# The first layer's FFN down with seven products for eight, its sum turned by TensorE, and another order of the last products

## The chip, the cores and the metric

The kernel runs on one core of a Trainium2 chip. The metric is the device time of one execution, in microseconds. The profile gives the engines these names: PE is TensorE (its loads of the stationary operand are PEld), DVE is VectorE, ACT is ScalarE, POOL is GpSimd, SP is SyncE, which here only issues DMAs.

## What is computed

Two layers of a decoder trunk on one sequence of 512 tokens with 1024 features. Each layer mixes four branches (a gated convolution, sparse attention, a gated recurrence, attention into 256 memory tokens), adds the result to `x`, and then applies an FFN:

```python
hf = rmsnorm(x, norm_ffn)
gate, up = jnp.split(hf @ ffn_w_up, 2, axis=-1)
return x + (jax.nn.silu(gate) * up) @ ffn_w_down
```

`ffn_w_up` is 1024 x 5632, `ffn_w_down` is 2816 x 1024. The change is in the last product, `(...) @ ffn_w_down`: a matrix of 512 tokens x 2816 times one of 2816 x 1024. Its 2816 rows are 22 K tiles of 128.

## The kernel before

**Products.** Each operand is split into a hi part, which TensorE's f32r format holds, and a lo part, the rest. A product of two operands is three matmuls (`mm3`, lines 275 to 277): hi x hi, hi x lo, lo x hi, added up in one bank of PSUM. ACT makes the hi part (line 97, the helper `A`), DVE the lo part (line 230 in `Chunk`, line 1068 in `split`). The tiles `w_hi` and `w_lo` have three buffers of 128 x 1024 (`W_BUFS`), the raw weights `w_raw` two. SP's queue loads the raw weights. PSUM's eight banks are three `mm`, three `tr` and two `at`.

**Who sets the order.** The program is written in one order, and a planner (the scheduler of the tile framework) puts each engine's instructions into an order of its own, by a timeline that it computes, by priorities (`tc.high_priority`), and by the dependences between tiles. Each engine then works strictly in that order. `tc.add_manual_dep(..., order, ...)` adds an order without a wait; `follow` (line 1058) uses it.

**The FFN** (`ffn`, from line 1172) goes in two parts of its 11 blocks of 256 hidden features: blocks 0 to 5, then 6 to 10 (`parts`). For each block, `features` multiplies eight K tiles of `h` with the gate's and the up's weights (96 matmuls of 128 x 512), DVE scales what comes out of PSUM (line 1208, `fg` and `fu`), ACT applies Silu, DVE multiplies (line 1211). When a part has its blocks, its share of the down product follows.

**Down, first layer** (`add_down`, line 1032). The hidden features are kept feature-major as `a_hi` and `a_lo` (lines 1215 and 1216). For each two chunks of 128 output features (`m0`) the weights of the part's K tiles are loaded and split, and `features` multiplies them: output features on the partitions, 512 tokens along the row. The sum in PSUM is added to a chunk of `x` that POOL's queue has brought back from DRAM (`x_c`, lines 1181 and 1043), and ACT's queue stores it (line 1046). That is done in both parts, 22 x 8 x 3 matmuls in all. In the second part each chunk at once becomes the next layer's `h` (`h_chunk`: hi part on ACT, lo part on DVE, line 289, and the squares' sum `ssq`, line 297).

**Down, last layer** (`down`, from line 1104). Here two K tiles form a 2 x 2 block problem: the two K tiles against the two halves of the tokens, and the two K tiles against the two halves of the output features. Eight block products become seven (a Strassen-Winograd scheme). `operands` (line 1085) makes seven combinations of 128 x 256 from a block's two feature tiles; `weight_sums` (line 1073) makes four combinations of a K pair's weights: POOL's queue loads the pair into `w_raw7` (line 1076), DVE does four subtractions (lines 1079 to 1082), POOL's queue stores them to `wt_dram` (line 1083), from which SP loads them again (lines 1132 and 1157). The hidden features are the stationary operand, so tokens come out on the partitions, and the result is added into the token-major `acc` (128 x 4 x 1024) by DVE (`evict`, line 1241). `x` enters `acc` beforehand, turned by TensorE (`x_in`, line 1190).

`down` runs in three stretches over the part's pairs. In the last one each pair `k` has a product into `ba` (two banks `mm`, called "main" below) and one into `bc` (two banks `at`), from one split of two weights:

```python
prod(ba, k, S3, p7, False, k == n - 1, True)
late.append((bc, k, S4, p3, False, k == n - 1, True))
if not n - 3 <= k < n - 1:
    for q in late:
        prod(*q)
    late = []
```

So as written, the products into `bc` of the pairs n-3, n-2 and n-1 come after the last product into `ba`; in the trace of before the planner has put each pair's behind its own main product. Then `evict` empties `ba` twice (into two halves of `acc`) and `bc`; in the last part of the last layer those of `bc` go out in halves of 256 columns, each followed by its transfer to the output (line 1244).

Of the kernel before, what the change touches and what calls it, by code (L numbers as in the profile page):

```python
# [21 lines left out]
P = 128  # L22
# [47 lines left out]
def hybrid_trunk(ctx: ExitStack, tc: tile.TileContext, x, mem, positions, norm_mix, w_in, conv_w,  # L70
# [41 lines left out]
    def f(ap):  # L112
        return ap.bitcast(F32)
# [127 lines left out]
    def wchunk(src, kt, n):  # L241
        return Chunk(src, kt, n)
# [29 lines left out]
    def mm3(ps, a, b, first, last, more=False):  # L272
        ah, al = a
        bh, bl = b
        pe.matmul(ps, ah, bh, start=first, stop=False, skip_group_check=more)  # L275
        pe.matmul(ps, ah, bl, start=False, stop=False, skip_group_check=more)  # L276
        pe.matmul(ps, al, bh, start=False, stop=last, skip_group_check=more)  # L277

    x_dram = nc.dram_tensor("x_spill", [P, KD, S], F32, kind="Internal").ap()
    wt_dram = nc.dram_tensor("w_sums", [P, FF // 256, 4, 512], F32, kind="Internal").ap()  # L280
# [751 lines left out]
    def add_down(x_chunk, w2d, a, kt, h2, ssq2, gain):  # L1032
        for m0 in range(0, KD, 2):
            ws = [(k0, wchunk(w2d[k0 * P:min(k0 + 8, kt) * P, m0 * P:(m0 + 2) * P], min(8, kt - k0), 256))
                  for k0 in range(0, kt, 8)]
            xs = [x_chunk(m0 + j) for j in range(2)]
            pss = [mm_ps() for _ in range(2)]
            for js in ([range(2)] if m0 + 2 < KD else [[0], [1]]):
                for k0, w in ws:
                    features(w, a, js, k0, kt, [pss[j] for j in js])  # L1040
            for j, xc in enumerate(xs):
                m = m0 + j
                dve.tensor_add(xc, xc, pss[j])
                if h2 is not None:
                    h_chunk(h2, ssq2, m, gain(m), xc)
                nc.scalar.dma_start(x_dram[:, m, :], xc)
# [26 lines left out]
    def weight_sums(fp, w2d, i):  # L1073

        raw = fp.tile([P, 4, 512], F32, name="w_raw7")
        nc.gpsimd.dma_start(raw.rearrange("p (e c) n -> p e (c n)", e=2),
                            w2d[2 * i * P:2 * (i + 1) * P, :].rearrange("(e p) n -> p e n", p=P))
        b12, b11, b22, b21 = (raw[:, j, :] for j in range(4))
        dve.tensor_sub(b11, b12, b11)
# [3 lines left out]
        nc.gpsimd.dma_start(wt_dram[:, i], raw)  # L1083

    def operands(fp, g0, g1):

        hi, lo = (fp.tile([P, 7, HALF], F32R, name=nm, bufs=6) for nm in ("a_hi", "a_lo"))
# [16 lines left out]
    def down(fp, w2d, sums, ops, evict):  # L1104
# [49 lines left out]
        for i0 in range(0, n, 2):  # L1154
# [17 lines left out]
    def ffn(l, h, ssq):  # L1172
# [3 lines left out]
        parts = ((0, 6), (6, n_f))  # L1176

        with tc.tile_pool(name="ffn", bufs=1, reuse_waits="tile") as fp:
# [14 lines left out]
            h2 = ssq2 = None  # L1193
            for part, (f0, f1) in enumerate(parts):
                ops = []
                if not last:
                    kt = 2 * (f1 - f0)
                    a = (fp.tile([P, 12, S], F32R, name="a_hi")[:, :kt], fp.tile([P, 12, S], F32R, name="a_lo")[:, :kt])
                if last:
                    weight_sums(fp, ffn_w_down[l], f0)  # L1200
                for fc in range(f0, f1):
# [10 lines left out]
                    if not last:  # L1212
                        for j, g in enumerate(gs):
                            i = 2 * (fc - f0) + j
                            A(a[0][:, i, :], g, AF.Copy)
                            dve.tensor_sub(a[1][:, i, :], g, f(a[0][:, i, :]))
                        continue
# [9 lines left out]
                if not last:  # L1227
                    if final:
                        h2, ssq2 = new_h(), new_ssq()
                    add_down(x_chunk, wd, a, kt, h2, ssq2, lambda c: g_mix(l + 1, c))  # L1230
                    continue
# [15 lines left out]
                down(fp, wd, wt_dram[:, f0:f1], ops, evict)  # L1247
        return h2, ssq2
# [34 lines left out]
```

## Time and profile before

| what | value |
|---|---|
| median of three runs | 2037.27 us (2035.32 to 2040.52) |
| the profiled execution | 2037.88 us |
| its span in the profile | 2036.2 us |
| mean granted TensorE clock | 0.997 |
| PE busy | 2017.4 us |
| DVE busy | 1356.6 us |
| ACT busy | 1046.3 us |
| first layer's FFN, first up product to the next layer's first product | 696.52 to 1056.54 us |
| last layer's FFN, first up product to the end of its products | 1680.70 to 2029.97 us |

The span runs from the first to the last instruction or transfer of one profiled execution; the time of that execution holds 1.7 us more. Rows of groups read: line, engine, operation, output tile from input tiles, shapes, count, then busy time in all, mean duration in ns, and idle time before. Rows of a timeline read: start in us, duration in us, engine, line, operation, tiles, shapes, count, and in brackets the idle time before it with what ended it.

### The profile page before, as it was taken

The page shows a single profiled execution, that of the slowest core. Times are in us where ns is not written, and L with a number is a line of the kernel's source. Part 1 is how long each engine was busy: PE and PEld are TensorE (multiplying, and loading weights), DVE is VectorE, ACT ScalarE, POOL GpSimd, SP SyncE. Part 2 cuts the span into 40 slices and gives each one's busy share as a digit, 9 for nine tenths or more (in the row PEclk, how much of TensorE's full clock was granted, in tenths as well). Part 3 has the DMA queues.
Part 4 walks back from the last instruction along what each step waited for, and adds up shares of the span by engine and source line. Part 5 has one row for each costly group of instructions (what it writes and reads, how often), then busy time and mean ns, then how long its engine had stood idle before and what let it go on. Part 6 is the DMA issues. An engine that isn't in the chain of part 4 may idle for free.

```text
span 2036.2 us, 26441 instructions
## 1 busy us (share of the span) xinstructions
PE 2017.4 (99%) x10090; PEld 1692.7 (83%) x10090; DVE 1356.6 (67%) x2653; ACT 1046.3 (51%) x1880; POOL 34.7 (2%) x75
## 2 busy tenths in 40 slices
PE   8999999999999999999999999999999999999998
PEld 8998987778888888888889898877888788888887
DVE  5768898647676554334446899855678566666665
ACT  7653654766665433222346455477667544333333
POOL 0000000000000000000000000000000000000000
PEclk9999999999999999999999999999999999999999
DMA  7623232222233532442262322222222445565654
GB/s 251 216 87 104 68 104 62 83 63 89 77 124 104 166 100 86 131 158 84 79 206 70 93 79 94 73 94 67 79 83 80 149 140 191 189 211 201 216 171 155
DMA packets 193470, 248.09 MB, mean 122 GB/s; under 512 B 5550, under 2 KB 166912, under 8 KB 191552
## 3 DMA queue, kind: packets, MB, share of 16 engines
q1 hardware_dynamic: 179584, 201.43, 31.2%
q0 software_dynamic: 6464, 30.02, 4.0%
q10 hardware_dynamic: 7296, 14.97, 1.9%
q8 instruction: 79, 1.29, 0.3%
q14 instruction: 47, 0.39, 0.1%
HBM read 218.08 MB, written 28.31 MB: 121 GB/s over the span
## 4 chain that ended last, share of the span: by engine, by line
PE 93%; DMA 3%; DVE 2%; ACT 1%; issue 1%; SPq 0%; DVEq 0%; ACTq 0%
PE mm L275 28%; PE mm L276 27%; PE mm L277 27%; DMA w_raw<-in_ffn_w_down_dram 1%; PE tr L732 1%; PE at L702 1%; PE tr L726 1%; DMA w_sums<-w_raw 1%; PE at L703 1%; PE at L275 1%; PE at L277 1%; PE at L276 1%; DMA w_raw<-in_mem_w_kv_dram 1%; PE tr L275 0%; PE tr L276 0%
## 5 line engine op out<-in xcount | busy, mean ns | idle before, releaser
L275 PE MATMUL mm<-h_hi,w_hi 128*128 128x512 f32 x1664 | 651.5, 393 | 0.9 <-DVE fg L1208 0.6
L276 PE MATMUL mm<-h_lo,w_hi 128*128 128x512 f32 x1664 | 652.3, 392 | 0.0
L277 PE MATMUL mm<-h_hi,w_lo 128*128 128x512 f32 x1664 | 649.3, 392 | 0.0
L97 ACT ACTIVATE w_hi<-w_raw 128x1024 fp32r<-128x1024 f32 (+2 forms) x368 | 381.5, 1039 | 410.0 <-PE mm L276 313.1
L230 DVE TENSOR_TENSOR w_lo<-w_raw,w_hi 128x1024 fp32r<-128x1024 f32 (+1 forms) x324 | 392.4, 1213 | 282.3 <-ACT w_hi L97 281.4
L275 PEld LDWEIGHTS mm<-h_hi,w_hi 128*128 128x128 f32 x1664 | 313.1, 188 | 66.0 <-DVE fg L1208 1.8
L277 PEld LDWEIGHTS mm<-h_hi,w_lo 128*128 128x128 f32 x1664 | 312.9, 188 | 64.5 <-issue 0.6
L276 PEld LDWEIGHTS mm<-h_lo,w_hi 128*128 128x128 f32 x1664 | 313.0, 188 | 64.0 <-issue 0.6
L276 PE MATMUL mm<-w_lo,h_hi 128*128 128x256 f32 (+2 forms) x368 | 109.2, 297 | 0.0
L277 PE MATMUL mm<-w_hi,h_lo 128*128 128x256 f32 (+2 forms) x368 | 109.2, 297 | 0.0
L275 PE MATMUL mm<-w_hi,h_hi 128*128 128x256 f32 (+2 forms) x368 | 108.6, 298 | 0.0
L275 PE MATMUL mm<-y_hi,w_hi 128*128 128x512 f32 x256 | 100.3, 394 | 1.2 <-ACT y_hi L97 1.2
L276 PE MATMUL mm<-y_lo,w_hi 128*128 128x512 f32 x256 | 100.5, 392 | 0.0
L277 PE MATMUL mm<-y_hi,w_lo 128*128 128x512 f32 x256 | 100.2, 392 | 0.0
L97 ACT ACTIVATE a_hi<-fg 128x512 fp32r<-128x512 f32 (+1 forms) x66 | 39.3, 596 | 111.0 <-DVE fg L1211 96.6
L97 ACT ACTIVATE prob<-prob,small 128x256 f32<-128x256 f32 (+3 forms) x128 | 69.0, 555 | 16.4 <-DVE small L715 9.1
L1068 DVE TENSOR_TENSOR w_lo<-w_raw,w_hi 128x1024 fp32r<-128x1024 f32 (+1 forms) x44 | 47.6, 1090 | 37.1 <-ACT w_hi L97 37.1
L276 PEld LDWEIGHTS mm<-w_lo,h_hi 128*128 128x128 f32 x368 | 70.1, 191 | 2.2
L277 PEld LDWEIGHTS mm<-w_hi,h_lo 128*128 128x128 f32 x368 | 70.1, 191 | 1.9
L275 PEld LDWEIGHTS mm<-w_hi,h_hi 128*128 128x128 f32 x368 | 69.8, 191 | 1.9
L275 PE MATMUL mm<-a_hi,w_hi 128*128 128x512 f32 x176 | 68.5, 389 | 0.0
L276 PE MATMUL mm<-a_lo,w_hi 128*128 128x512 f32 x176 | 68.5, 389 | 0.0
(401 smaller groups left out, 3208.9 us busy)
## 6 DMA issues: line engine op xcount, KB each, us to landing
w_raw<-in_w_in_dram SPq DMA_DIRECT2D x72, 1024.0 KB, 5.2
w_raw<-in_ffn_w_up_dram SPq DMA_DIRECT2D x44, 1024.0 KB, 5.1
w_raw<-in_w_lift_dram SPq DMA_DIRECT2D x32, 512.0 KB, 3.5
w_raw<-in_ffn_w_down_dram SPq DMA_DIRECT2D x13, 1024.0 KB, 5.0
w_raw<-in_ffn_w_down_dram POOLq DMA_DIRECT2D x11, 1024.0 KB, 6.1
w_sums<-w_raw POOLq DMA_DIRECT2D x11, 1024.0 KB, 5.2
w_raw<-w_sums SPq DMA_DIRECT2D x11, 768.0 KB, 5.7
w_raw<-in_mem_w_kv_dram SPq DMA_DIRECT2D x8, 1024.0 KB, 5.4
```

The source lines that it names most:

```text
L97: i = act.activation(dst, src, func, **kw)
L230: dve.tensor_sub(lo, raw[:, k:e], f(hi))
L275: pe.matmul(ps, ah, bh, start=first, stop=False, skip_group_check=more)
L276: pe.matmul(ps, ah, bl, start=False, stop=False, skip_group_check=more)
L277: pe.matmul(ps, al, bh, start=False, stop=last, skip_group_check=more)
L702: pe.matmul(ps, q[:, hh, s], k[0][:, :n], start=True, stop=False)
L703: pe.matmul(ps, q[:, hh, s], k[1][:, :n], start=False, stop=True)
L726: pe.transpose(pp[:, (2 * e + i) * P:(2 * e + i + 1) * P], probs[2 * i + e][:, b * P:(b + 1) * P], ident)
L732: pe.matmul(pv[e * HD:(e + 1) * HD, :], vt[:, b, :], pt[:, b, e * 2 * P:(e + 1) * 2 * P], start=b == 0, stop=b == t)
L1068: follow(dve.tensor_sub(lo[:, k:k + n, :], src, f(hi[:, k:k + n, :])), earlier)
```

## The change

- `parts` of the first layer becomes three: blocks 0 to 4, blocks 5 to 8, and, called plain, blocks 9 and 10. The first two parts go through `operands`, `weight_sums` and `down` as in the last layer, with five buffers of operands in place of six, into an `acc` that POOL sets to zero. That is 9 pairs of K tiles, 18 of 22.
- The plain part (4 K tiles) only splits its hidden features into hi and lo, and goes through `add_down` once for the whole layer. There, after the products of a chunk, four `pe.matmul` in plain f32 with `acc` as the stationary operand and the identity as the moving one add the turned sum into the same bank of PSUM. `x_c` is loaded, added to and stored once for each chunk, not twice. `add_down` takes its weights in one chunk of 4 K tiles x 256 for each `m0`.
- `wt_dram` has room for both layers.
- In `down`, in both layers, the products into `bc` of the pairs n-3 to n-1 are written as all of token tile 0, then all of token tile 1, and `follow` binds each of them behind the last main product.

```diff
-    def add_down(x_chunk, w2d, a, kt, h2, ssq2, gain):
+    def add_down(x_chunk, w2d, a, kt, acc, h2, ssq2, gain):
+
         for m0 in range(0, KD, 2):
-            ws = [(k0, wchunk(w2d[k0 * P:min(k0 + 8, kt) * P, m0 * P:(m0 + 2) * P], min(8, kt - k0), 256))
-                  for k0 in range(0, kt, 8)]
+            w = wchunk(w2d[:, m0 * P:(m0 + 2) * P], kt, 256)
             xs = [x_chunk(m0 + j) for j in range(2)]
             pss = [mm_ps() for _ in range(2)]
             for js in ([range(2)] if m0 + 2 < KD else [[0], [1]]):
-                for k0, w in ws:
-                    features(w, a, js, k0, kt, [pss[j] for j in js])
+                features(w, a, js, 0, kt, [pss[j] for j in js])
+                for j in js:
+                    for t in range(NT):
+                        pe.matmul(pss[j][:, t * P:(t + 1) * P], acc[:, t, (m0 + j) * P:(m0 + j + 1) * P], ident,
+                                  start=False, stop=True, skip_group_check=True)
...
-    def operands(fp, g0, g1):
-
-        hi, lo = (fp.tile([P, 7, HALF], F32R, name=nm, bufs=6) for nm in ("a_hi", "a_lo"))
+    def operands(fp, g0, g1, plain, n_ops):
+
+        hi, lo = (fp.tile([P, 7, HALF], F32R, name=nm, bufs=n_ops) for nm in ("a_hi", "a_lo"))
+        if plain:
+            for o, g in ((0, g0), (2, g1)):
+                h_, l_ = (x[:, o:o + 2, :].rearrange("p a b -> p (a b)") for x in (hi, lo))
+                A(h_, g, AF.Copy)
+                dve.tensor_sub(l_, g, f(h_))
+            return hi, lo
...
-        def prod(bank, i, o, b, start, stop, more=False):
+        def prod(bank, i, o, b, start, stop, more=False, tiles=(0, 1)):
             hi, lo = ops[i]
-            for t, ps in enumerate(bank):
+            made = []
+            for t in tiles:
                 s = slice(t * P, (t + 1) * P)
-                mm3(ps, (hi[:, o, s], lo[:, o, s]), b, start, stop, more)
+                made += mm3(bank[t], (hi[:, o, s], lo[:, o, s]), b, start, stop, more)
+            return made
...
-                prod(ba, k, S3, p7, False, k == n - 1, True)
+                main = prod(ba, k, S3, p7, False, k == n - 1, True)
                 late.append((bc, k, S4, p3, False, k == n - 1, True))
-                if not n - 3 <= k < n - 1:
-                    for q in late:
-                        prod(*q)
-                    late = []
+                if k < n - 3:
+                    prod(*late.pop())
+        for t in range(2):
+            for q in late:
+                for i in prod(*q, tiles=(t,)):
+                    follow(i, main[-1:])
...
-        parts = ((0, 6), (6, n_f))
+        parts = ((0, 6, False), (6, n_f, False)) if last else ((0, 5, False), (5, 9, False), (9, n_f, True))
...
-                    ops.append(operands(fp, *gs))
-                    if fc == 0:
+                    ops.append(operands(fp, *gs, plain, 6 if last else 5))
+                    if acc is None:
                         acc = fp.tile([P, NT, D], F32, name="acc")
-                    if fc in (1, 3):
+                        if not last:
+                            pool.memset(acc, 0.0)
+                    if last and fc in (1, 3):
                         x_in(2 * fc - 2)
-                    if fc + 1 < f1:
-                        weight_sums(fp, ffn_w_down[l], fc + 1)
-                final = part == len(parts) - 1
+                    if not plain and fc + 1 < f1:
+                        weight_sums(fp, l, fc + 1)
+                final = last and part == len(parts) - 1
...
+                if plain:
+                    h2, ssq2 = new_h(), new_ssq()
+                    add_down(x_chunk, wd, [Pairs(t) for t in zip(*ops)], 2 * len(ops), acc, h2, ssq2,
+                             lambda c: g_mix(l + 1, c))
+                    return h2, ssq2
```

`Pairs` only gives `features` the plain operands by K tile. `mm3` now returns its three matmuls, and `weight_sums` takes the layer in place of the weights.

More of the change, by code (lines that the diff above doesn't have):

```diff
@@ L274, in mm3 @@
         bh, bl = b
-        pe.matmul(ps, ah, bh, start=first, stop=False, skip_group_check=more)
-        pe.matmul(ps, ah, bl, start=False, stop=False, skip_group_check=more)
-        pe.matmul(ps, al, bh, start=False, stop=last, skip_group_check=more)
+        return [pe.matmul(ps, ah, bh, start=first, stop=False, skip_group_check=more),
+                pe.matmul(ps, ah, bl, start=False, stop=False, skip_group_check=more),
+                pe.matmul(ps, al, bh, start=False, stop=last, skip_group_check=more)]
     x_dram = nc.dram_tensor("x_spill", [P, KD, S], F32, kind="Internal").ap()
-    wt_dram = nc.dram_tensor("w_sums", [P, FF // 256, 4, 512], F32, kind="Internal").ap()
+    wt_dram = nc.dram_tensor("w_sums", [DEPTH, P, FF // 256, 4, 512], F32, kind="Internal").ap()
     kv_dram = [nc.dram_tensor(f"kv{l}", [P, 4, 2, 2, MEM], F32, kind="Internal").ap() for l in range(DEPTH)]
@@ L1030, in residual, with __init__, __getitem__ @@
                 nc.scalar.dma_start(x_dram[:, m, :], xT[:, m, :])
-    def add_down(x_chunk, w2d, a, kt, h2, ssq2, gain):
+    class Pairs:
+        def __init__(self, tiles):
+            self.tiles = tiles
+        def __getitem__(self, at):
+            _, k, s = at
+            return self.tiles[k // 2][:, k % 2 * 2:k % 2 * 2 + 2, :].rearrange("p a b -> p (a b)")[:, s]
+    def add_down(x_chunk, w2d, a, kt, acc, h2, ssq2, gain):
         for m0 in range(0, KD, 2):
-            ws = [(k0, wchunk(w2d[k0 * P:min(k0 + 8, kt) * P, m0 * P:(m0 + 2) * P], min(8, kt - k0), 256))
-                  for k0 in range(0, kt, 8)]
+            w = wchunk(w2d[:, m0 * P:(m0 + 2) * P], kt, 256)
             xs = [x_chunk(m0 + j) for j in range(2)]
@@ L1043, in add_down @@
                 dve.tensor_add(xc, xc, pss[j])
-                if h2 is not None:
-                    h_chunk(h2, ssq2, m, gain(m), xc)
+                h_chunk(h2, ssq2, m, gain(m), xc)
                 nc.scalar.dma_start(x_dram[:, m, :], xc)
@@ L1071, in hybrid_trunk, with weight_sums @@
     SUM3, SUM1, SUM2, SUM4 = range(4)
-    def weight_sums(fp, w2d, i):
+    def weight_sums(fp, l, i):
         raw = fp.tile([P, 4, 512], F32, name="w_raw7")
         nc.gpsimd.dma_start(raw.rearrange("p (e c) n -> p e (c n)", e=2),
-                            w2d[2 * i * P:2 * (i + 1) * P, :].rearrange("(e p) n -> p e n", p=P))
+                            ffn_w_down[l][2 * i * P:2 * (i + 1) * P, :].rearrange("(e p) n -> p e n", p=P))
         b12, b11, b22, b21 = (raw[:, j, :] for j in range(4))
@@ L1191, in x_in @@
                     A(acc[:, :, (m0 + m) * P:(m0 + m + 1) * P], ps.rearrange("p (a b) -> p a b", b=P), AF.Copy)
-            h2 = ssq2 = None
-            for part, (f0, f1) in enumerate(parts):
+            acc = None
+            for part, (f0, f1, plain) in enumerate(parts):
                 ops = []
[L1196 to L1200, printed above, removed]
+                if not plain:
+                    weight_sums(fp, l, f0)
                 for fc in range(f0, f1):
@@ L1245, in evict @@
                     return adds
-                down(fp, wd, wt_dram[:, f0:f1], ops, evict)
-        return h2, ssq2
+                down(fp, wd, wt_dram[l, :, f0:f1], ops, evict)
+        return None, None
     for l in range(DEPTH):
```

13 lines of the change are left out of this document (1 added, 12 removed).

## The prediction

> **What bounds the kernel now.** I read the page first, then the windows of the two FFNs, then who waits there, then the single instructions.
>
> ```profile
> span 2036.2 us, 26441 instructions
> ...
> PE 2017.4 (99%) x10090; PEld 1692.7 (83%) x10090; DVE 1356.6 (67%) x2653; ACT 1046.3 (51%) x1880; POOL 34.7 (2%) x75
> ...
> PE 93%; DMA 3%; DVE 2%; ACT 1%; issue 1%; SPq 0%; DVEq 0%; ACTq 0%
> ```
>
> PE is busy nearly always and is 93% of the chain that ended last. The change is in layer 0's FFN, where the old products run; layer 1's FFN already has the seven products. Each is one window, from its first up product to the start of what follows its last product (columns: window, length, PE, PEld, DVE, ACT, POOL busy, clock, DMA share, GB/s):
>
> ```profile
> 696.52:1056.54 360.02, 359.84 (x1587) 297.60 (x1586) 160.97 (x190) 111.63 (x135) 9.16 (x17) 1.00 0.38 120
> 1680.70:2029.97 349.27, 348.90 (x1553) 288.25 (x1551) 229.31 (x307) 132.12 (x167) 15.48 (x25) 1.00 0.55 190
> ```
>
> The products that these windows hold (one of the three lines of `mm3`, the others have the same counts), and all that PE waited for in each:
>
> ```profile
> L275 PE MATMUL mm<-h_hi,w_hi 128*128 128x512 f32 x352 | 137.1, 389 | 0.2 <-DVE fg L1208 0.2
> ...
> L275 PE MATMUL mm<-a_hi,w_hi 128*128 128x512 f32 x176 | 68.5, 389 | 0.0
> ```
> ```profile
> L275 PE MATMUL mm<-w_hi,a_hi 128*128 128x512 f32 x88 | 28.2, 389 | 0.0
> ...
> L275 PE MATMUL at<-w_hi,a_hi 128*128 128x512 f32 x44 | 14.0, 389 | 0.0
> L275 PE MATMUL tr<-w_hi,a_hi 128*128 128x512 f32 x22 | 8.6, 389 | 0.0
> ...
> L1190 PE MATMUL tr<-ident,w_raw 128*128 128x128 f32 x32 | 4.1, 272 | 0.0
> ```
> ```profile
> PE mm L275 <- DVE fg L1208: 0.2, 1, 0.2
> ```
> ```profile
> PE mm L275 <- DVE fg L1208: 0.4, 2, 0.2
> ```
>
> A duration of 389 ns is not a price, since products overlap. The price is the distance from start to start:
>
> ```profile
> 1000.10 0.39 PE L275 MATMUL mm<-h_hi,w_hi 128*128 128x512 f32 x1
> 1000.33 0.39 PE L276 MATMUL mm<-h_lo,w_hi 128*128 128x512 f32 x1
> 1000.56 0.39 PE L277 MATMUL mm<-h_hi,w_lo 128*128 128x512 f32 x1
> 1000.78 0.39 PE L275 MATMUL mm<-h_hi,w_hi 128*128 128x512 f32 x1
> ```
>
> Three in 0.68 us: 0.2267 us each. Layer 0: 3 x (352 + 176) = 1584 products, and two of the norm, times 0.2267 is 359.5 of the 360.02 us. Nothing but the number of products sets this stage. Layer 1 has 3 x (352 + 154) = 1518: its down takes 462 where layer 0's takes 528.
>
> **The change, part by part.**
>
> *Products, layer 0.* Before: 22 K tiles x 8 chunks x 3 = 528. After: nine pairs of K tiles at 7 products x 2 token tiles x 3 = 42 make 378, and the last four K tiles, done as before, 96: 474. 54 fewer x 0.2267 = **-12.24 us**.
>
> *Turning the sum.* 4 x 8 = 32 calls of `pe.matmul` on plain f32, 128x128 by 128 columns. L954 is the same form (16 calls a layer, 32 in all):
>
> ```profile
> L954 PE MATMUL at<-cmr,zf x64: 270/275/275, 471.0 to 1579.9; 128*128 128x128 f32 x64
> ```
> ```profile
> 471.01 1.06 PE L954 MATMUL at<-cmr,zf 128*128 128x128 f32 x8
> 472.00 0.68 PE L956 MATMUL at<-q_mid,k_mid 128*64 128x64 f32 x8
> ```
>
> A call is two records. Eight records take 1.06 us, the last 0.275 of it: (1.06 - 0.275) / 7 = 0.112 us a record; to the next group it would be 0.99 / 8 = 0.124. So 64 records cost 7.2 to 7.9; I take **+7.2**, the step inside a run. Two thirds of the gain goes here.
>
> *Switching between forms.* After twelve short transposes the distance between two long products is once longer:
>
> ```profile
> 1725.22 1.47 PE L1190 MATMUL tr<-ident,w_raw 128*128 128x128 f32 x12
> 1726.45 0.48 PE L275 MATMUL mm<-h_hi,w_hi 128*128 128x512 f32 x1
> 1726.77 0.40 PE L276 MATMUL mm<-h_lo,w_hi 128*128 128x512 f32 x1
> ```
>
> 0.32 for 0.227: 0.09 a group. `add_down` has five groups (three m0 with one, the last with two): **+0.45**; none at best, 2.9 if every call stands alone.
>
> *Order of the last products.* The new rule puts 18 late products (into `at`) behind all into `mm`, nine for token tile 0, then nine for tile 1. At the kernel's end, before:
>
> ```profile
> 2028.80 2.48 DVE L1241 TENSOR_TENSOR acc<-acc,mm 128x512 f32<-128x512 f32 x4 [4.48 <-PE mm L277]
> ...
> 2029.74 0.39 PE L277 MATMUL at<-w_hi,a_lo 128*128 128x512 f32 x1
> ...
> 2031.20 1.41 DVE L1241 TENSOR_TENSOR acc<-acc,at 128x256 f32<-128x256 f32 x4
> 2031.98 1.01 ACTq L1244 DMA_DIRECT2D out_dram<-acc  x2
> ```
>
> The four additions out of `mm` are late: they occupy DVE until 2031.28, and the four halves out of `at` end at 2032.61, though PE was done at 2030.13 (its last start and 0.39). After: `mm` is done 18 x 0.2267 = 4.1 us before PE's end, so its 2.48 us of additions are over by 2028.6, and tile 0's two halves (0.35 each) by 2029.4; only tile 1's two halves (0.70) follow PE's end. DVE ends near 2030.86: **-1.75**. The transfers behind stay the same.
>
> But the order also holds buffers. `w_hi`/`w_lo` have three; the three late pairs of weights occupy all until tile 1's products. The first is free six products before the end (1.36 us; 1.2 us when its last product's own 0.39 has run out). What the next up stage then has to do:
>
> ```profile
> 2022.00 1.06 ACT L97 ACTIVATE w_hi<-w_raw 128x1024 fp32r<-128x1024 f32 x1 [0.97 <-PE at L277]
> ```
> ```profile
> 2023.10 1.23 DVE L1068 TENSOR_TENSOR w_lo<-w_raw,w_hi 128x1024 fp32r<-128x1024 f32 x1 [0.81 <-ACT w_hi L97]
> ```
>
> 2.33 us from free to `w_lo` ready, so it is ready about 1.2 us after the last late product. Two products need `w_hi` alone (0.45): a wait of 0.77 at each of three ends of `down` (two in layer 0, one in layer 1). Queued behind PE's wait is the whole next up stage, and DVE and ACT with it. The planner shortens such a wait by starting the second bank with its hi products:
>
> ```profile
> 1056.54 0.39 PE L275 MATMUL mm<-h_hi,w_hi 128*128 128x512 f32 x1
> 1056.77 0.39 PE L276 MATMUL mm<-h_lo,w_hi 128*128 128x512 f32 x1
> 1057.00 0.39 PE L275 MATMUL mm<-h_hi,w_hi 128*128 128x512 f32 x1
> ```
>
> That takes off another 0.45: 0.3 each, **+0.9** (0 to 2.4). With four pairs only, the last split comes up to 0.3 late too: into the range.
>
> *What I cost at nothing.* DVE gains 36 subtractions of weights, 32 additions into `acc`, and the additions of the operands; it loses 8 additions into `x_c`. Layer 1's window carries more of the same (11 pairs) at 229 of 349 us, with PE waiting 0.4. The queues: SP loses 16 weight loads of `add_down` and gets four back, and gains 24 or so smaller ones of `down`; POOL gains nine loads and nine stores of sums and loses eight loads of `x_c`; ACT loses eight stores. Layer 1's window has these too, at a DMA share of 0.55, and PE waited there for no load. If that cover went, a load of weights would show in full, some 5 us each: that is the last rival's kind. New to both is the memset of `acc` on POOL, eight times this one:
>
> ```profile
> L879 POOL MEMSET a_intra<- 128x512 f32 x4 | 2.0, 525 | 0.0
> ```
>
> 8 x 0.525 = 4.2 us, some 100 us before its first reader. POOL's next load of sums stands behind it, with 22 us (96 products) to the next pair. Should it keep DVE from emptying a bank, a bank may wait 5.44 us (24 products): nothing. In `add_down` an m0 shrinks to 24 x 0.2267 + 16 x 0.112 = 7.2 us:
>
> ```profile
> L1043 DVE TENSOR_TENSOR x_c<-x_c,mm x16: 680/688/689, 841.9 to 1057.4; 128x512 f32<-128x512 f32 x16
> ...
> L289 DVE SCALAR_TENSOR_TENSOR h_lo<-x_c,prm,h_hi x8: 744/748/755, 1017.1 to 1059.1; 128x512 fp32r<-128x512 f32 x8
> ...
> DMA to landing us min/median/max: 2.0/4.0/7.0
> ```
>
> DVE per m0: twice (0.69 + 0.75 + about 0.69 for the squares) and one lo half of 1.23: 5.5 of 7.2. An `x_c` buffer comes back through addition and ACT (about 2.4), store (4.0), POOL and load (4.5): 10.9 within two m0, 14.4. With both transfers at 7.0 it is late by 2.5, twice: 5 us at most, into the range.
>
> **Sum**: -12.24 + 7.2 + 0.45 + 0.9 - 1.75 = -5.4. The profiled execution took 2037.88 (its span and 1.7 around it), so 2032.4; the median of the three runs is 0.6 lower: **2031.8**.
>
> **Rivals.**
>
> *No new wait.* The planner fills everything and layer 1's mixer, whose order is planned anew, loses its one long wait:
>
> ```profile
> PE mm L275 <- ACT y_hi L97: 1.2, 1, 1.2
> ```
>
> -5.4 - 0.9, and up to 1.2 more: 2029.7 to 2030.9, 2030.3 in the middle. For it: PE waited for little anywhere; against: that mixer's order was the same planner's before.
>
> *The held buffers cost full price*, three times 0.77 and the late split 0.3, or the `x_c` trip in part: 2034. For it: 2.33 against 1.2 us. Against: the planner's filling.
>
> *PE's count is not the bound.* Then the 12.24 and the 7.2 don't show, and the tail alone does: 2035.5. Against it: the two windows differ by 10.75 us, where the count gives 66 x 0.2267, less 32 short transposes at 0.109 ((1.47 - 0.272) / 11), less four switches at 0.09 and one wait of 0.45: 10.7. [...]
>
> *Slower: DVE stands before a load.* DVE works in order; a subtraction of `weight_sums` that waits for POOL's load blocks the emptying of banks behind it:
>
> ```profile
> DVE w_raw L1079 <- DMA w_raw<-in_ffn_w_down_dram: 20.1, 8, 6.1
> ```
>
> At worst 6.1 + four subtractions of 0.69, less the 5.44 a bank can wait: 3.4 us a pair. Nine pairs are new; from two at that price it is slower than before, with four 2045. Against: layer 1's eight such waits cost PE one of 0.2 us (0.45 with its restart).
>
> **Chances.** Forecast (2030.8 to 2033) 0.46; no new wait 0.20; held buffers 0.18; not the bound 0.05; DVE before a load 0.11. What a measurement of this kernel can tell from no change is about 0.3%, 6.1 us, so faster means under 2031.2: all of the second and 0.20 of the forecast, 0.40. Slower means over 2043.4: 0.07 of the last. The rest is 0.53. The range leaves out the last rival and a little below: 2029.5 to 2036.5.
>
> **What would show it.** 10100 products on PE (54 fewer, 64 more); layer 0's window near 356.5 us; L954's spacing on the new line, in five groups; starts 0.3 us late after the three downs; DVE's last addition 0.8 us after PE's last product, not 2.5. Wrong if PE waits in layer 0's FFN for `fg` or `x_c` by more than 2 us, or if the turning records lie further apart than 0.124.

## The result, and the profile after

The changed kernel takes 2032.23 us (median of nine runs, 2031.15 to 2033.42) against 2037.27 (nine runs, 2035.32 to 2040.52) on the same chip: a ratio of 0.9975 [0.9966, 0.9983], 0.25% less. The interval lies below 1, so the gain is there, but it is smaller than the 0.3% from which the prediction calls a kernel faster. The profiled execution took 2033.14 us, 4.74 less than that of before. The first lines of its page and of its chain of what ended last:

```profile
span 2031.4 us, 26667 instructions
...
PE 2015.5 (99%) x10100; PEld 1691.8 (83%) x10100; DVE 1427.8 (70%) x2774; ACT 1067.9 (53%) x1914; POOL 45.0 (2%) x86
...
PE 95%; DVE 2%; DMA 2%; ACT 1%; issue 0%; DVEq 0%; SPq 0%; ACTq 0%
```

PE has the 10100 products that were counted, and is the chain still, 95% of it where it was 93%; DMA's share has gone from 3% to 2%. DVE is busy 71 us more, nearly all of it beside PE. Where the time went is told by windows: layer 0's FFN, the stretch from there to layer 1's FFN (called "the mixer": layer 1's mixer and its residual), and layer 1's FFN (columns as before):

```profile
697.22:1053.51 356.29, 355.55 (x1598) 294.21 (x1596) 232.84 (x311) 135.33 (x169) 13.77 (x23) 1.00 0.52 179
1053.51:1677.56 624.05, 622.23 (x3242) 523.29 (x3241) 458.12 (x989) 376.82 (x733) 2.54 (x9) 1.00 0.29 93
1677.56:2027.44 349.88, 348.98 (x1553) 288.17 (x1551) 231.56 (x311) 131.72 (x167) 15.30 (x25) 1.00 0.56 193
```

Layer 0's FFN is 3.73 us shorter (360.02 before). The mixer is the same (1680.70 - 1056.54 = 624.16 before). Layer 1's FFN, whose number of products hasn't changed, is 0.61 longer. From the end of the products to the end of the span it is 3.99 us (2031.43 - 2027.44), 6.22 before: 2.23 less. The FFN begins 0.70 later than before, with nothing changed ahead of it; over all the profiles of this study that start lies between 694.2 and 697.2 us, so stages are compared by their lengths.

The turning of the sum, one row for its 64 records and some of its groups:

```profile
L1051 PE MATMUL mm<-ident,acc x64: 270/275/275, 1032.3 to 1053.5; 128*128 128x128 f32 x64
```
```profile
1032.30 1.95 PE L1051 MATMUL mm<-ident,acc 128*128 128x128 f32 x16
1034.00 0.48 PE L276 MATMUL mm<-a_lo,w_hi 128*128 128x512 f32 x1
1034.31 0.40 PE L277 MATMUL mm<-a_hi,w_lo 128*128 128x512 f32 x1
1034.55 1.05 PE L1051 MATMUL mm<-ident,acc 128*128 128x128 f32 x8
1035.36 0.48 PE L275 MATMUL mm<-a_hi,w_hi 128*128 128x512 f32 x1
```

A record costs (1.95 - 0.275) / 15 = 0.112 us, as L954's did. The planner made six groups (16, 8, 8, 16, 8, 8), not five. A group of eight takes 0.81 us to the next long product, and that product one step 0.08 longer (0.31 for 0.227): 0.89 us, which is 8 x 0.112. The switch was in the step already; the prediction paid it twice. POOL's memset takes 3.55 us where 4.2 were expected, and is far from anything that reads it:

```profile
L1234 POOL MEMSET acc<- x1: 3549/3549/3549, 658.1 to 658.1; 128x4096 f32 x1
```

What PE waited for, in layer 0's FFN and then in layer 1's:

```profile
PE mm L277 <- DVE w_lo L230: 0.5, 1, 0.5
PE mm L275 <- DVE fg L1226: 0.2, 1, 0.2
```
```profile
PE mm L275 <- ACT w_hi L97: 0.7, 1, 0.7
PE mm L275 <- DVE fg L1226: 0.2, 1, 0.2
```

The new waits stand where they were expected, behind the three ends of `down`. The list gives only a part of their cost, since it counts neither the longer step before a wait nor the restart after it. Measured as start distances beyond 0.2267 us, they cost 0.83 us at 855 (0.07 and 0.65 before the product that waits, 0.11 after it), 0.41 at 981 and 1.05 at 1870. The first of them, from the timeline (PE's weight loads left out):

```profile
853.44 2.01 ACT L97 ACTIVATE w_hi<-w_raw 128x1024 fp32r<-128x1024 f32 x2 [5.74 <-PE at L277]
...
853.77 0.68 DVE L1093 TENSOR_TENSOR w_raw<-w_raw 128x512 f32<-128x512 f32 x1
...
854.37 0.68 DVE L1255 TENSOR_TENSOR acc<-acc,at 128x512 f32<-128x512 f32 x1
...
854.60 0.46 PE L275 MATMUL mm<-h_hi,w_hi 128*128 128x512 f32 x1
...
854.97 1.22 DVE L230 TENSOR_TENSOR w_lo<-w_raw,w_hi 128x1024 fp32r<-128x1024 f32 x1
855.13 0.40 PE L275 MATMUL mm<-h_hi,w_hi 128*128 128x512 f32 x1
...
855.37 0.39 PE L276 MATMUL mm<-h_lo,w_hi 128*128 128x512 f32 x1
...
856.24 0.50 PE L277 MATMUL mm<-h_hi,w_lo 128*128 128x512 f32 x1 [0.49 <-DVE w_lo L230]
```

ACT could start `w_hi` only when a late product had let go of a buffer, and PE filled in with the four products that need `w_hi` alone, both as predicted. But ACT's first `w_hi` is ready near 854.5, and DVE begins `w_lo` at 854.97: a subtraction of the next part's `weight_sums` (L1093) and an eviction stood before it. DVE had been late since the first of those subtractions, which stood 0.48 us before POOL's load of the weights, and was busy without a pause from there on:

```profile
849.45 0.69 DVE L1090 TENSOR_TENSOR w_raw<-w_raw 128x512 f32<-128x512 f32 x1 [0.48 <-DMA w_raw<-in_ffn_w_down_dram]
```

And the end of the kernel:

```profile
2023.10 2.48 DVE L1255 TENSOR_TENSOR acc<-acc,mm 128x512 f32<-128x512 f32 x4 [1.31 <-PE mm L277]
...
2025.60 0.75 DVE L1255 TENSOR_TENSOR acc<-acc,at 128x256 f32<-128x256 f32 x2
...
2027.21 0.39 PE L277 MATMUL at<-w_hi,a_lo 128*128 128x512 f32 x1
2027.63 0.75 DVE L1255 TENSOR_TENSOR acc<-acc,at 128x256 f32<-128x256 f32 x2 [1.29 <-PE at L277]
```

The four additions out of `mm` are over by 2025.58 and those of token tile 0 by 2026.35, beside the late products. DVE ends at 2028.38, 0.78 us behind PE (2027.60); before it was 2.48.

### The profile page after: what moved, and what is told of

Same layout as the page of the kernel before. It is cut to its first block, busy times and chain, and to the rows that moved or that the text cites. A ratio compares the mean times of both kernels' runs of the same rounds, so it can differ in the third digit from the quotient of the medians.

```text
span 2031.4 us, 26667 instructions
## 1 busy us (share of the span) xinstructions
PE 2015.5 (99%) x10100; PEld 1691.8 (83%) x10100; DVE 1427.8 (70%) x2774; ACT 1067.9 (53%) x1914; POOL 45.0 (2%) x86
## 4 chain that ended last, share of the span: by engine, by line
PE 95%; DVE 2%; DMA 2%; ACT 1%; issue 0%; DVEq 0%; SPq 0%; ACTq 0%
PE mm L275 28%; PE mm L277 27%; PE mm L276 27%; PE tr L732 1%; PE at L702 1%; PE tr L726 1%; PE at L703 1%; PE at L277 1%; PE at L276 1%; PE at L275 1%; DVE acc L1255 1%; PE tr L275 1%; PE tr L277 1%; PE tr L276 1%; DMA w_raw<-in_ffn_w_down_dram 1%; ACT w_hi L97 0%
## 5 line engine op out<-in xcount | busy, mean ns | idle before, releaser
L97 ACT ACTIVATE w_hi<-w_raw 128x1024 fp32r<-128x1024 f32 (+1 forms) x384 | 394.9, 1033 | 391.5 <-PE mm L276 248.5
L230 DVE TENSOR_TENSOR w_lo<-w_raw,w_hi 128x1024 fp32r<-128x1024 f32 x304 | 369.4, 1218 | 203.9 <-ACT w_hi L97 202.8
L1079 DVE TENSOR_TENSOR w_lo<-w_raw,w_hi 128x1024 fp32r<-128x1024 f32 (+1 forms) x80 | 86.4, 1090 | 64.9 <-ACT w_hi L97 64.8
L97 ACT ACTIVATE a_hi<-fg 128x512 fp32r<-128x512 f32 (+1 forms) x84 | 48.5, 580 | 109.1 <-DVE fg L1229 81.8
L97 ACT ACTIVATE gate_e<-gate 128x512 f32<-128x512 f32 x64 | 40.2, 628 | 45.2 <-DVE gate L534 44.6
L276 PE MATMUL mm<-w_lo,a_hi 128*128 128x512 f32 x160 | 62.2, 389 | 0.0
```

Of the source, the lines that this page charges most:

```text
L97: i = act.activation(dst, src, func, **kw)
L230: dve.tensor_sub(lo, raw[:, k:e], f(hi))
L1079: follow(dve.tensor_sub(lo[:, k:k + n, :], src, f(hi[:, k:k + n, :])), earlier)
```

## The experiments

The theory: PE's count of products times 0.2267 us, plus 7.2 for the turning, sets layer 0's FFN; the new order shortens the end and costs a wait at each end of `down`. The rivals: the count is not the bound; or the price lies with DVE. The table gives stage lengths from one profile each, the median, and the ratio to the kernel before in runs on the same chip.

| kernel | layer 0's FFN | mixer | layer 1's FFN | end | median | ratio |
|---|---|---|---|---|---|---|
| before | 360.02 | 624.16 | 349.27 | 6.2 | 2037.27 | 1 |
| after | 356.29 | 624.05 | 349.88 | 4.0 | 2032.23 | 0.9975 [0.9966, 0.9983] |
| e1, seven products, old order | 355.01 | 624.10 | 348.75 | 6.4 | 2031.89 | 0.9976 [0.9968, 0.9985] |
| e2, new order alone | 360.04 | 624.22 | 350.09 | 3.7 | 2035.94 | 0.9996 [0.9987, 1.0005] |
| e3, new order in the last `down` only | 354.94 | 624.10 | 348.79 | 4.0 | 2029.66 | 0.9964 [0.9952, 0.9977] |
| e7, two pairs late | 355.48 | 624.10 | 348.79 | 4.6 | 2030.70 | 0.9968 [0.9955, 0.998] |
| e12, sums written later | 356.05 | 624.08 | 349.83 | 4.0 | 2030.97 | 0.9973 [0.9962, 0.9983] |
| e10, e3 with six plain K tiles | 356.28 | 624.09 | 348.76 | 4.0 | 2030.95 | 0.9967 [0.9955, 0.998] |
| e4, turned by `transpose` | 352.40 | 633.22 | 349.85 | 4.0 | 2037.16 | 1.0001 [0.9992, 1.001] |
| e5, sum not turned | 349.01 | 633.22 | 349.87 | 4.0 | 2033.51 | 0.9982 [0.9973, 0.999] |
| e6, e3 and e4 | 351.99 | 633.24 | 348.76 | 4.0 | 2035.44 | 0.9992 [0.9983, 1.0001] |
| e9, e6, squares on POOL | 351.59 | 633.62 | 348.74 | 4.0 | 2035.15 | 0.9988 [0.9979, 0.9996] |
| e11, e6, turned twice | 355.18 | 634.38 | 348.79 | 4.0 | 2039.16 | 1.0011 [1.0002, 1.002] |
| e8, e6 with six plain K tiles | 353.28 | 624.00 | 348.75 | 4.0 | 2027.51 | 0.995 [0.9938, 0.9962] |

### The two halves of the change apart

**e1**, the change with the old order of the last products:

```diff
-                if k < n - 3:
-                    prod(*late.pop())
-        for t in range(2):
-            for q in late:
-                for i in prod(*q, tiles=(t,)):
-                    follow(i, main[-1:])
+                if not n - 3 <= k < n - 1:
+                    for q in late:
+                        prod(*q)
+                    late = []
```

> The change with the old order of the last products. Theory (PE's count sets the time, the new order shortens the end and adds waits): 54 products fewer and 64 turning records give -5.0; no shorter end (+2.2 against the change), no waits behind the three downs (-2.3): about 2032 us, as the change itself, with the first layer's FFN window at 355 us. Rival (the count is not the bound, the gain is the end's): about 2037 us. Rival (the waits come with the third part, not with the order): 2034.5 us, the waits still there.

**e2**, the kernel before with those lines (and the `tiles` of `prod`) exchanged the other way.

> The kernel before with the new order of the last products alone, which touches the last layer's two downs. Theory: the end is 2.2 us shorter, one wait of about 1.0 us comes behind the last layer's first down: 2036.1 us. Rival (the held buffers cost nothing by themselves, the waits need the first layer's new load): 2035.0 us and no wait. Rival (the order does nothing): 2037.3 us.

Measured: e1 2031.89 us, e2 2035.94. The windows of both FFNs in e1, and what PE waited for in layer 0's:

```profile
696.42:1051.43 355.01, 354.83 (x1598) 294.54 (x1596) 233.00 (x311) 135.50 (x169) 13.77 (x23) 1.00 0.53 180
1675.53:2024.28 348.75, 348.56 (x1553) 288.35 (x1551) 229.87 (x307) 131.86 (x167) 15.30 (x25) 1.00 0.56 190
```
```profile
PE mm L275 <- DVE fg L1224: 0.2, 1, 0.2
```

Without the new order all three waits are gone (355.01 for 356.29, 348.75 for 349.88), and the long end is back (6.4 for 4.0). 1.28 + 1.13 = 2.41 us lost inside, 2.4 won at the end: the order is worth nothing as a whole, and the seven products alone give all that the change gives. e2 shows the same from the other side: 2.5 won at the end, and a wait of 1.27 us in layer 1, where an old one of 0.45 is gone.

### The order only where it pays

**e3**: only the very last `down` uses the new order, the others the old one. **e7**: only the last two pairs are late, everywhere, so that a third buffer comes free earlier.

```diff
-                if k < n - 3:
+                if final and k < n - 3:
                     prod(*late.pop())
+                if not final and not n - 3 <= k < n - 1:
+                    for q in late:
+                        prod(*q)
+                    late = []
```
```diff
-                if k < n - 3:
+                if k < n - 2:
```

> The change with the new order only in the very last down. Theory (three held buffers make the waits): the three waits go (-2.3), the short end stays: about 2030 us. Rival (the waits come from subtractions of weights or from banks): they stay, about 2032 us.

> The change with two pairs' late products behind the last main product instead of three. Theory: the third buffer of w_hi and w_lo is free some 5 us before the end of a down, the three waits go (-2.3); at the kernel's end the additions out of mm have 2.7 us of products beside them, not 4.1, and the last addition comes up to 0.6 later: about 2030.4 us. Rival (not the buffers): waits stay, 2032.5 us.

Measured: e3 2029.66 us, e7 2030.70. e3 has both gains and no wait; its layer 0 takes 354.94. e7 keeps a wait of 0.47 us (by start distances) at 854, and its end is 0.6 us longer than e3's. That wait is DVE's: the first `w_hi` is ready at 852.55, no buffer holds it up, but four subtractions and four evictions keep DVE from `w_lo` until 853.67. So without the new order there is no wait, and with a third buffer free only what DVE makes is left; the second layer's last `down` needs no new order anywhere else to have its short end. e3 beats before; against after its interval overlaps, and what sets it apart is the windows, 2.4 us shorter in all.

### Is the rest of the wait DVE's subtractions?

**e12**: the later part's first `weight_sums` is written behind the first block's products of that part, not ahead of them.

```diff
-                if not plain:
+                if not plain and not f0:
                     weight_sums(fp, l, f0)
...
+                    if not plain and f0 and fc == f0:
+                        weight_sums(fp, l, f0)
```

> The change with a later part's first weight_sums written behind the products of that part's first block, so that its four subtractions no longer stand on DVE between the last additions of a down and the first lo half of the next block. Theory (of the waits behind the downs 0.3 to 0.4 is the held buffers', the rest DVE's subtractions, since the one down with no sums behind it costs 0.4): the waits of 0.8 and 1.05 shrink to about 0.4, -1.0: 2031.2 us. Rival (the buffers make all of it): waits as in the change, 2032.2 us.

Measured: 2030.97 us, no difference from after that the intervals show; the waits are 0.61, 0.41 and 1.04 us, for 0.83, 0.41 and 1.05. As an experiment this told little: the planner put the same subtractions ahead of `w_lo` again in both layers, so nothing was taken away. What answers the question is a series over the ends of `down` in the new order at which PE goes through the same five products. Behind after's second `down` no sums follow, and DVE is free when ACT is done:

```profile
979.45 2.96 ACT L97 ACTIVATE w_hi<-w_raw 128x1024 fp32r<-128x1024 f32 x3 [5.51 <-DVE acc L1255]
...
980.54 1.23 DVE L230 TENSOR_TENSOR w_lo<-w_raw,w_hi 128x1024 fp32r<-128x1024 f32 x1 [1.09 <-ACT w_hi L97]
```

One `w_hi` takes 1.06 us, so the first is ready at 980.51, and `w_lo` starts 0.03 later. Elsewhere subtractions and evictions stand before `w_lo`, and the delay is longer:

| place | DVE's wait for the load before its subtractions | DVE's delay, `w_hi` ready to `w_lo` begun | PE's wait in all |
|---|---|---|---|
| after, second `down` | no subtractions | 0.03 | 0.41 |
| e5, first `down` | 0.21 | 0.20 | 0.56 |
| e12, first `down` | 0.25 | 0.24 | 0.61 |
| e4, first `down` | 0.35 | 0.34 | 0.71 |
| after, first `down` | 0.48 | 0.47 | 0.83 |
| e2, layer 1 | 1.35 | 0.90 | 1.27 |

Each wait is DVE's delay and 0.36 to 0.38 us. So the held buffers cost about 0.37 at each place, close to the 0.3 of the prediction, and the rest is DVE's other work in front of `w_lo`. How late that work is goes back to a load: in the four first `down`s DVE's delay is, to 0.01 us, the time that DVE stood before POOL's load of the next part's weights, and from the end of that stand to `w_lo` it is 5.52 or 5.53 us each time, without a pause. In e2 the subtraction that waits for the load stands last before `w_lo`, and the load came 0.29 us after `w_hi` was ready. In after's layer 1 it is again 5.53 us from the load:

```profile
1865.32 0.69 DVE L1090 TENSOR_TENSOR w_raw<-w_raw 128x512 f32<-128x512 f32 x1 [1.01 <-DMA w_raw<-in_ffn_w_down_dram]
```

No run started that load earlier. In that place the delay is 1.0 us, and the wait 1.05 and not 1.4: the planner moved two more products ahead there, and the first of them waits for the third `w_hi` on ACT.

### What the turning costs

**e4** turns the sum by `pe.transpose` into a bank of its own, and DVE adds it to `x_c` ahead of the products. **e5** leaves the turning out. **e6** is e3 with e4's edit.

```diff
             xs = [x_chunk(m0 + j) for j in range(2)]
+            for j, xc in enumerate(xs):
+                ps = tr_ps()
+                for t in range(NT):
+                    pe.transpose(ps[:, t * P:(t + 1) * P], acc[:, t, (m0 + j) * P:(m0 + j + 1) * P], ident)
+                dve.tensor_add(xc, xc, ps)
...
-                for j in js:
-                    for t in range(NT):
-                        pe.matmul(pss[j][:, t * P:(t + 1) * P], acc[:, t, (m0 + j) * P:(m0 + j + 1) * P], ident,
-                                  start=False, stop=True, skip_group_check=True)
```

> The change with the sum turned by pe.transpose into tr banks, ahead of a chunk's products, and added into x_c by DVE. Theory (turning is on the path at 0.112 us a record): 32 records in place of 64, -3.6: about 2028.6 us. Rival (DVE becomes the bound of add_down: eight more additions, 6.9 us a step where PE needs 6.3): PE waits there up to 2.4 us, about 2031 us. Rival (the turning hides): 2032 us.

> The change without the turning: the share of the nine pairs in the first layer's output is left out. Theory: the whole 7.2 us go, about 2025 us, the window of the first layer's FFN 349 us. Rival (add_down is held by DVE or by the x_c loads, not by PE): 2028 us or more, with PE waiting in add_down.

> New order only at the very end, and turning by transposes: both edits together. Theory: -2.3 and -3.6 add up: about 2026.4 us. Rival (each frees time that the other's wait takes): 2028 us or more.

Measured: 2037.16, 2033.51 and 2035.44 us, all three far from what was expected. Layer 0's FFN did what the count says. Less their waits (1.24, 0.97 and 0.86 us) after takes 355.05, e5 348.04 and e4 351.54: the turning costs 7.0 us by matmul and 3.5 by transpose. (e5 has two longer steps in `add_down`, 0.26 and 0.34 us up to 1031.10, that its list of waits doesn't show; with these 0.15 us taken off too the two prices are 7.2 and 3.7.) But the mixer, which none of these edits touches, is 9.2 us longer. The two windows of e5, and what PE waited for in its mixer:

```profile
695.48:1044.49 349.01, 348.55 (x1533) 287.11 (x1532) 230.27 (x308) 132.60 (x167) 13.79 (x23) 1.00 0.53 179
1044.49:1677.71 633.22, 626.95 (x3239) 525.25 (x3238) 460.94 (x993) 379.44 (x735) 2.55 (x9) 0.99 0.30 94
```
```profile
PE at L702 <- DVE small L715: 2.9, 1, 2.9
PE mm L275 <- ACT y_hi L97: 1.2, 1, 1.2
PE mm L275 <- ACT unit L97: 1.1, 2, 0.9
PE tr L793 <- DVE twin L791: 0.8, 1, 0.8
PE mm L275 <- DVE gate L553: 0.3, 1, 0.3
```

After's mixer has only three of these (1.2, 0.3 and 0.3). Idle time grew by (633.22 - 626.95) - (624.05 - 622.23) = 4.45 us, which is these waits. The other 4.7 are busy time: the same products took longer. PE around the long wait, and the granted clock of two stretches there:

```profile
1311.92 0.39 PE L277 MATMUL tr<-w_hi,h_lo 128*128 128x512 f32 x1
1315.18 0.48 PE L702 MATMUL at<-k_hi,qS 128*128 128x128 f32 x1 [2.87 <-DVE small L715]
...
1318.36 0.63 PE L276 MATMUL mm<-h_lo,w_hi 128*128 128x512 f32 x1
1318.79 0.63 PE L275 MATMUL mm<-h_hi,w_hi 128*128 128x512 f32 x1
1319.21 0.63 PE L276 MATMUL mm<-h_lo,w_hi 128*128 128x512 f32 x1
```
```profile
1311.00:1312.30 1.30, 1.30 (x6) 0.75 (x4) 1.23 (x4) 1.09 (x2) 0.00 (x0) 1.00 0.00 0
1315.10:1321.80 6.70, 6.62 (x20) 5.45 (x21) 4.85 (x18) 3.71 (x15) 0.00 (x0) 0.50 0.16 34
```

After 2.87 us of idle the clock is at 0.50 for 6.7 us, and products lie 0.427 us apart where they lay 0.2267: by estimate half of the 6.7, 3.35 us, lost on top of the 2.87. (The 2.87 us count from the end of the product before, 1311.92 + 0.39.) So by this estimate the one wait costs 6.2 us. 1.4 us of the longer busy time isn't accounted for.

### Why the mixer became slower

Three theories: the additions of e4 and the like make DVE late (then less work for DVE in `add_down` mends it); the shorter steps of `add_down` do (then longer steps mend it); or only the order that the planner wrote for the mixer counts. **e9** is e6 with six of the seven additions of squares on POOL. **e11** is e6 with 32 more transposes, whose result nobody uses. **e8** is e6, and **e10** e3, with blocks 8 to 10 plain in place of 9 and 10.

```diff
-            dve.tensor_add(ssq, ssq, sq)
+            adder.tensor_add(ssq, ssq, sq)
...
-                h_chunk(h2, ssq2, m, gain(m), xc)
+                h_chunk(h2, ssq2, m, gain(m), xc, pool if m < KD - 1 else dve)
```
```diff
+                spare = tr_ps()
+                for t in range(NT):
+                    pe.transpose(spare[:, t * P:(t + 1) * P], acc[:, t, (m0 + j) * P:(m0 + j + 1) * P], ident)
```
```diff
-        parts = ((0, 6, False), (6, n_f, False)) if last else ((0, 5, False), (5, 9, False), (9, n_f, True))
+        parts = ((0, 6, False), (6, n_f, False)) if last else ((0, 5, False), (5, 8, False), (8, n_f, True))
```

> As e6, but POOL adds up seven of the eight squares in add_down instead of DVE, 1.4 us a step less for DVE (5.5 where PE needs 6.3). Theory (DVE's load in add_down delays the next layer): mixer back at 624 us, about 2026 us. Rival (PE's shorter step itself, or POOL's slower additions, delay the sum of squares that the norm waits for): the mixer stays near 633 us, about 2035 us.

> As e6, but every chunk is turned a second time into a tr bank that nobody reads: 32 more records on PE, so that a step of add_down takes PE 7.2 us as in the change, against 6.9 on DVE. Compared by their written order, PE's instructions of the second mixer stand here as in e9 and e4 (62% of the lines in the place that they have in the change), not as in e8 or e10 (99%). Theory (the mixer is long because the planner wrote another order for it, whatever comes late on the chip): the mixer stays at 633 us, the window of the first layer's FFN is 355.5: 2039 us. Rival (the mixer is long because a short step of add_down makes the next layer's h late on the chip): mixer 624 us, 2030 us, faster than with one turning.

> As e6 (new order only at the end, turning by transposes), but with three plain blocks in place of two: 8 pairs with seven products, 6 K tiles through add_down. Theory (in add_down DVE needs 6.9 us a step where PE needed 6.3, so the next layer's h comes late, and the next mixer is planned and run with waits, 633 us for 624): a step now has 36 products and takes PE 9.0 us where DVE needs 7.5, the mixer takes 624 us again, and PE has 32 records fewer (-3.6) and 6 products more (+1.4) than with the new order at the end alone: about 2027.5 us. Rival (the mixer's longer plan has nothing to do with add_down's cover): 2036 us.

> As e3 (new order only at the end, turning by matmuls), but with three plain blocks in place of two. Theory (PE's count): 6 products more, +1.4: about 2031 us, the first layer's FFN window 1.4 us longer than in e3, the mixer at 624 us. Rival (the third down of that size costs more in waits than it saves): 2029.7 us or less.

Measured: e9 2035.15, e11 2039.16, e8 2027.51 and e10 2030.95 us. e9's mixer is as long as e6's (633.62), but e9 settles little: DVE's operations beside POOL's additions took longer (`h_lo` 0.97 us in the median, 0.74 in after), and DVE's busy time in that window stayed (234.87 us for 234.27 in e6). e11's steps are longer by 3.2 us in all, which by the count gives PE 7.2 us a step where DVE needs 6.9, and its mixer is no shorter (634.38): neither the length of the step nor a DVE that falls behind it on the chip is the cause. e8's is back at 624.00 with the same transposes and additions:

```profile
695.10:1048.38 353.28, 352.98 (x1571) 291.88 (x1570) 229.34 (x307) 129.97 (x163) 12.52 (x21) 1.00 0.50 169
1048.38:1672.38 624.00, 622.18 (x3239) 523.45 (x3238) 461.17 (x993) 379.89 (x736) 2.54 (x9) 1.00 0.30 95
```

Compared in the traces, place by place (the 62% and 99% of e11's expectation are of the written order), before, e1, e2, e3, e7, e8, e10 and e12 have 97% or more of PE's 3238 instructions in layer 1's mixer where after has them, and their mixers take 624 us; e4, e5, e6, e9 and e11 have 54 to 57%, and theirs take 633 to 634. So the mixer comes in an order near after's or in another one, and a change upstream decides which the planner writes. In the longer one PE comes to L702 (in e5) while DVE still has selections (L841, L842) ahead of the L715 that PE waits for. What in the plan tips it stays open: e8 and e6 differ in one block more of plain work, and no run shows which of the planner's estimates that shifts. e10 confirms the count once more: six products more than e3, 356.28 - 354.94 = 1.34 us, where 6 x 0.2267 is 1.36.

e8 is the fastest: 0.995 [0.9938, 0.9962] of before, with the cheap turning and the order of e3: against e6 its six products more cost 1.3 us, and its mixer is 9.2 us shorter.

## Why the prediction was right

2031.8 us was forecast, 2032.23 measured; 2029.5 to 2036.5 holds it, and "within 0.3%" had the largest chance. By its steps:

| step | predicted | measured | from |
|---|---|---|---|
| 54 products fewer | -12.24 | -12.0 | e5 less its waits, 348.04, for 360.02 |
| turning, with the switches | +7.65 | +7.0 | after less e5, both less their waits |
| waits behind `down`, layer 0 | +0.6 | +1.24 | 0.83 and 0.41 |
| wait behind `down`, layer 1 | +0.3 | +0.6 | 1.05, and 0.45 of an old wait gone |
| the end | -1.75 | -2.23 | 3.99 for 6.22 |
| sum | -5.4 | -5.4 | |

That the sum of the stages is right to a tenth is luck, because the errors cancel: the prediction had 0.4 too little gained by the first two steps, 0.9 too little paid for waits, 0.5 too little gained at the end. The first two rows are read by e5; its pause of 0.15 us would make them -12.1 and +7.2. e1, which has no waits, gives their sum without e5: 355.01 - 360.02 = -5.01. Layer 0's window of 356.5 doesn't follow from the prediction's own terms, which give 356.0; it was 356.29. Between the profiles lie 4.74 us (0.70 of later start, 0.11 of mixer), between the medians 5.04.

- **The bound.** PE's start distance times its count gave the windows of this study: 12.0 us for 54 products (12.24 counted), 1.34 for six (1.36). The rival by which the count is not the bound is out.
- **Turning.** The step inside a run was the right price (0.112). The switch (+0.45) was counted on top of it and wasn't there.
- **Waits.** They came at the three places named, with the planner's filling. The size was off: 0.3 each was predicted, 0.41, 0.83 and 1.05 measured. Without DVE's delay it is 0.37; the prediction's own numbers give 0.68 for the full wait (2.33 less 1.2 less 0.45), not 0.77, and 0.23 after the filling. The prediction let DVE start `w_lo` when `w_hi` is ready; the subtractions of the next part's sums, which it listed under "what I cost at nothing", stood before it in two of the three (0.47 and 1.0 us), late by as much because of a load. The rival of held buffers at full price had the size of the three together (0.77 each, 2.31, for 2.29) but not the reason: the planner's filling was there, and DVE's delay made up for it.
- **The end.** DVE's 1.70 was the 1.75 of the prediction. "The transfers behind stay the same" failed, for a reason that no run shows: they take 3.05 us from DVE's end (2028.38 to 2031.43) for 3.57 before (2032.61 to 2036.18).
- **DVE before a load** came, in small and by another way than that rival's. No bank stayed full for it: the only PE wait by DVE's results beside `w_lo` is the old `fg` of 0.2. But the 0.48 and 1.01 us for which DVE stood before POOL's load came out as its delay in front of `w_lo`, and so as some 0.5 and 0.7 us of PE's waits (0.83 and 1.05 less 0.37).
- **The trip of `x_c`** cost nothing: PE waited for none.
- **What it didn't see** is what decides a neighbouring change: the order of a stage that the diff doesn't touch. Here it held, but that was luck too: "that mixer's order was the same planner's before" is no reason for it, since in five of the twelve variants it moved by 9 us, more than the whole gain.

## What to carry to other kernels

Where an engine is busy 99% and a stage's window is count times start distance, do the sum with the start distance, and give each removed or added instruction its price from it; here that was right to 0.24 of 12.24 us for 54 products, and to 0.02 for six. Put an order that holds buffers only where its gain is (here the last `down`), since elsewhere the next stage paid for it (2.41 us in the two FFNs). When a wait is longer than its cause explains, follow the late engine back through its own queue: here DVE's delay was made 5.5 us earlier, at a load. And where a planner writes the order, compare it in the stages that you didn't touch before you believe that an edit was bad: e4's edit won 3.9 us in its stage and lost 9.2 in another.

## What the runs showed of the hardware

- **An idle gap of 2.87 us on TensorE was followed by half the granted clock**, in e5 at 1315.1 for 6.7 us (0.50 there, 1.00 ahead of the gap): by the estimate above 6.2 us for a wait of 2.9. Layer 0's mixer has the same gap in before and in after, so it isn't peculiar to the variants. What follows is not always as long: over the 6.6 us behind the gap the clock is 0.54 in after and 0.74 in before, by estimate 3.0 and 1.7 us lost (6.6 x 0.46 and 6.6 x 0.26), in a stretch that the change doesn't touch. With the gap itself some 4.6 to 6 us lie there unused; no run tried to get them. No such fall was seen behind a gap of 1.17 us (the wait for `y_hi` in after, ended at 1599.03): the clock from 1599.00 to 1605.60 is 1.00. The gap and the clock in after, then the clock in before:

```profile
337.86 0.48 PE L702 MATMUL at<-k_hi,qS 128*128 128x128 f32 x1 [2.87 <-DVE small L715]
```
```profile
337.80:344.40 6.60, 6.54 (x20) 5.47 (x21) 4.83 (x17) 3.61 (x15) 0.00 (x0) 0.54 0.13 24
```
```profile
337.80:344.40 6.60, 6.20 (x23) 5.02 (x24) 4.76 (x17) 4.11 (x16) 0.00 (x0) 0.74 0.22 51
```

- **A turned 128x128 block of float32** costs two records of 0.112 us as a matmul with the identity (7.0 to 7.2 us for 32 blocks, the switches among them), and one of about 0.11 us as a transpose (3.5 to 3.7 us for 32).
- **POOL beside DVE**, in e9: POOL's additions of 128x512 took 1.75 us in the mean, and DVE's `h_lo` in the same stretch up to 1.79, with a median of 0.97 where it is 0.74 in after:

```profile
L297 POOL TENSOR_TENSOR ssq<-ssq,sq 128x512 f32<-128x512 f32 x6 | 10.5, 1754 | 134.4 <-ACT sq L97 134.3
```
```profile
L289 DVE SCALAR_TENSOR_TENSOR h_lo<-x_c,prm,h_hi x8: 740/968/1792, 1034.3 to 1054.1; 128x512 fp32r<-128x512 f32 x8
```
